# Moving the first loads of a one-layer decoder kernel: x's columns to another DMA queue, x's rows behind the second projection's weights

## The chip, the cores and the metric

The kernel runs on one core of one Trainium2 chip. The metric is the device time of one execution in microseconds (us), lower is better; it was run three times, and the median counts.

## The reference

One decoder layer on a sequence of 256 tokens with 1024 channels, in float32:

```python
h = rmsnorm(x, mix_norm_g)                       # x: (256, 1024)
proj = h @ w_in                                  # 1024 x 5632: qa ka va | qd kd vd | qm | three gates
qa, ka, qd, kd = rope(rmsnorm per head, positions)   # 64 wide heads; qm only normed
mem_n = rmsnorm(mem, mem_norm_g); mk, mv = mem_n @ w_mem_kv
o_a = block attention(qa, ka, va) @ w_branch_moba    # 6 heads
o_d = dilated attention(qd, kd, vd) @ w_branch_dil   # 6 heads
o_m = attention(qm, mk, mv) @ w_branch_mem           # 4 heads, 256 memory tokens
x = x + (sig(g0) * o_a + sig(g1) * o_d + sig(g2) * o_m) @ w_out
u = causal depthwise conv(rmsnorm(x) @ w_ffn_up)     # 1024 x 5632
x = x + (silu(u_gate) * u_val) @ w_ffn_down          # 2816 x 1024
```

The rotary part needs cos and sin of position times inverse frequency, and the dilated attention a table of counts, which is a constant.

## The kernel before

**Precision.** Every weight is read once, as float32, and split on the chip in two parts: `hi`, a rounded copy made on ACT, and `lo`, the remainder, made on DVE (some later on ACT with a DMA that accumulates). The activations are split the same way. A product is three matmuls: hi by hi, hi by lo, lo by hi.

**Columns and rows of x.** TensorE contracts over the partitions, so it needs x with channels on the partitions. The host gives x in that form too (`x_cols`, eight slabs `k` of 128 channels by 256 tokens, 128 KB each). `column_task` multiplies slab k with the norm's gain (ACT: `T_x` hi, DVE: `T_x` lo). The projections start from these and do without the mean square; that comes from the rows (`xs`, two tiles of 128 tokens, 512 KB each), squared and summed by `sums`, made into 1/rms by `rstd_task` (DVE, then POOL), and multiplied in afterwards: `head_scale_task` makes it for the head norms, `v_task` applies it as `va` and `vd` leave PSUM, and `row_scale_task` spreads it over all partitions with a matmul (`tp_Rx`) into `R`, which the gates take. `mem` goes the same way, with columns (`T_mem`) and rows.

**Weights.** They come in pieces through a ring of six raw buffers (`NRAW`): five pieces for `va` (one slab, one, two, two, two), four of 384 KB each for `vd`, `qa`, `ka` and so on, 512 KB for gates. `load` issues a piece on SP's queue as soon as the piece six before it is split. The order of the projections is written out in `ORDER`: va vd qa G0 ka G1 G2 mv mk ....

**Order.** A planner (`Order`) keeps an estimated clock for each engine, and issues next the stage that can start first by it, the one with the lower priority number among those close together. Each engine then runs its instructions in that order. `Stage("dve", 18.0)` means: not before 18 on the planner's clock. Where the planner expects TensorE to idle early on, `keep_busy` puts in small matmuls without use (`warm_...`, named by the time at which the planner expects the next one).

**First loads.** They are issued by hand, all on SP's queue, in the order of `LOADS`: x01 is slabs 0 to 1, `g` the gains, `w` the next weight piece, r0 and r1 the rows of x, `c` three loads: `cst` (the counts and the inverse frequencies), the positions and the head gains `hg`. What follows is planned: `mem_task` at 16 issues the convolution's weights, and mem's columns and rows; `rope_task` from 18 makes the rotary tables (19 small DVE operations on `rt`, three sines on ACT, then tables `ropeA` and `ropeB`); `mask_task` from 20.

Of the kernel before, what the change touches and what calls it, by code (L numbers as in the profile page):

```python
# [20 lines left out]
P = 128  # L21
# [16 lines left out]
RAW = 3  # L38
PRIO_SCALE = 11
CUTS = (0, 1, 2, 4, 8)  # L40
LOADS = "x01 g w x12 w x24 w x46 w x68 w r0 r1 c"
SUMS = (4, 130, 5)
BACK = (1.5, 2.0)
SLACK = 0.6
MEM_AT = 16.0
PRIO_SPLIT = (0, 0, 0, 12, 12, 22, 35, 40)
MAGIC = 12582912.0
TWO_PI = float(np.nextafter(np.float32(2.0 * np.pi), np.float32(0.0)))
# [185 lines left out]
def tile_layer(ctx: ExitStack, tc: tile.TileContext, io, out):  # L234
# [170 lines left out]


    xs = cpool.tile([P, NT, D], F32, tag="xs", name="xs")
    gcol = cpool.tile([P, 3, KT], F32, tag="gcol", name="gcol")
    cst = cpool.tile([P, 288], F32, tag="cst", name="cst")
    pos_i = cpool.tile([P, NT], I32, tag="pos_i", name="pos_i")  # L410
    hg = cpool.tile([P, 6, DH], F32, tag="hg", name="hg")
    conv = cpool.tile([P, 2 * NF, 4], F32, tag="conv", name="conv")
    ident = cpool.tile([P, P], F32, tag="ident", name="ident")
# [4 lines left out]
    maskf = cpool.tile([P, 512], F32, tag="maskf", name="maskf")  # L418
    A = cpool.tile([P, 4, NT, DH], F32, tag="ropeA", name="ropeA")
    B = cpool.tile([P, 4, NT, DH], F32, tag="ropeB", name="ropeB")  # L420
    cnt, invf = cst[:, 0:256], cst[:, 256:288]

    task = {}

# [35 lines left out]
    def head_scale_task(key, t):  # L460

        yield from rstd_task(key, t)
        rs = rstd[key, t]
        yield Stage("dve")
        dve.tensor_scalar(rs[:, 1:2], rs[:, 0:1], rs[:, 0:1], 1.0 / DH, op0=ALU.mult, op1=ALU.mult)
# [50 lines left out]


    def mask_task():
        yield Stage("dve", 20.0)
        dve.memset(maskf[:, 0:128], 0.0)  # L520
        dve.tensor_scalar(maskf[:, 128:256], cnt[:, 128:256], 0.0, NEG, op0=ALU.is_equal, op1=ALU.mult)
        dve.tensor_scalar(maskf[:, 256:512], cnt, 0.0, NEG, op0=ALU.is_equal, op1=ALU.mult)

    def rope_task():

        N = NT * HALF
        rt = apool.tile([P, 16, N], F32, tag="pT", name="rt", bufs=2)
        a, r, rc, sn, ns, cs, fr = (rt[:, k] for k in range(7))
        a12, acc, it, f0, f1 = (rt[:, k:k + 2].rearrange("p a n -> p (a n)") for k in (7, 9, 11, 13, 3))
        a1, a2 = rt[:, 7], rt[:, 8]  # L530
        posf = cpool.tile([P, NT], F32, tag="posf", name="posf")
        shape = [P, NT, HALF]
        yield Stage("dve", 18.0)
        dve.tensor_copy(posf, pos_i)
        yield Stage("dve")
        dve.tensor_mul(a.rearrange("p (t f) -> p t f", t=NT), invf.unsqueeze(1).to_broadcast(shape),
                       posf.unsqueeze(2).to_broadcast(shape))
        yield Stage("dve")
        dve.tensor_copy(a1.bitcast(F32R), a)
        yield Stage("dve")  # L540
        dve.tensor_sub(a2, a, a1)
        for d in range(3):
            yield Stage("dve")
            dve.tensor_scalar(it.bitcast(I32), a12, INV_2PI[d], None, op0=ALU.mult)
            yield Stage("dve")
            dve.scalar_tensor_tensor((acc, f0, f1)[d], a12, INV_2PI[d], it.bitcast(I32), op0=ALU.mult,
                                     op1=ALU.subtract)
        for f in (f0, f1):
            yield Stage("dve")
            dve.tensor_add(acc, acc, f)  # L550
        for d in (3, 4):
            yield Stage("dve")
            dve.scalar_tensor_tensor(acc, a12, INV_2PI[d], acc, op0=ALU.mult, op1=ALU.add)
        yield Stage("dve")
        dve.tensor_add(r, rt[:, 9], rt[:, 10])
        yield Stage("dve")
        dve.tensor_scalar(fr, r, MAGIC, MAGIC, op0=ALU.add, op1=ALU.subtract)
        yield Stage("dve")
        dve.tensor_sub(r, r, fr)
        yield Stage("dve")  # L560
        dve.tensor_scalar(rc, r, 0.25, None, op0=ALU.add)
        yield Stage("dve")
        dve.tensor_scalar(fr, rc, MAGIC, MAGIC, op0=ALU.add, op1=ALU.subtract)
        yield Stage("dve")
        dve.tensor_sub(rc, rc, fr)
        yield Stage("act")
        act.activation(ns, r, AF.Sin, scale=-TWO_PI)
        act.activation(sn, r, AF.Sin, scale=TWO_PI)
        act.activation(cs, rc, AF.Sin, scale=TWO_PI)
        yield Stage("dve")  # L570
        hq = hg.rearrange("p (a b) d -> p a b d", b=2)[:, :, 0, :]
        dve.tensor_scalar(hq, hq, DH ** -0.5, None, op0=ALU.mult)
        shape = [P, 4, NT, HALF]
        tab = {n: v.rearrange("p (t f) -> p t f", t=NT).unsqueeze(1).to_broadcast(shape)
               for n, v in (("cs", cs), ("sn", sn), ("ns", ns))}
        for hh in range(2):
            lo, hi = slice(hh * HALF, (hh + 1) * HALF), slice((1 - hh) * HALF, (2 - hh) * HALF)
            yield Stage("dve")
            dve.tensor_mul(A[:, :, :, lo], tab["cs"], hg[:, 0:4, lo].unsqueeze(2).to_broadcast(shape))
            yield Stage("dve")  # L580
            dve.tensor_mul(B[:, :, :, lo], tab["sn" if hh else "ns"], hg[:, 0:4, hi].unsqueeze(2).to_broadcast(shape))
# [476 lines left out]


    def mem_task():  # L1060
        yield Stage("pool", MEM_AT)
        nc.sync.dma_start(conv, io["conv"])
        cols = sig[:, KT:2 * KT, :]
        rows = sig[:, 2 * KT:3 * KT, :].rearrange("p a b -> p (a b)").rearrange("p (t n) -> p t n", t=NT)
        there = []
        for out_, in_ in [(cols[:, 0:4], io["mem_cols"][:, 0:4]), (cols[:, 4:8], io["mem_cols"][:, 4:8])] + \
                [(rows[:, t, :], io["mem"][t * P:(t + 1) * P, :]) for t in range(NT)]:
            nc.sync.dma_start(out_, in_)
            at["dma"] = max(at["dma"], od.t["pool"] + 1.15) + 1.5
            there.append(at["dma"] + 1.4)  # L1070
        columns_of("mem", 2, cols, 15, lambda k: there[k // 4])
        for t in range(NT):
            sums(rows[:, t, :], "mem", t, 16, [(0, 512, "act", there[2 + t]), (512, 1024, "act", there[2 + t])])
            task["rs", "mem", t] = od.add(head_scale_task("mem", t), 14)

    def keep_busy(start):

# [11 lines left out]
    with tc.manual_schedule():  # L1089
        nc.vector.memset(ones, 1.0)  # L1090
        nc.gpsimd.memset(mhalf, -0.5)
        warm = cpool.tile([P, 1], F32, tag="warm", name="warm")
        nc.scalar.activation(warm, mhalf[:, 0:1], AF.Square)
        xcol = sig[:, 0:KT, :]
        at["dma"] = 1.9
        there = {}
        for w in LOADS.split():
            if w == "g":
                nc.sync.dma_start(gcol, io["gcol"])
                at["dma"] += 0.06  # L1100
            elif w == "w":
                load(0.0, at["raw"] + 1)
            elif w == "c":
                nc.sync.dma_start(cst, io["cst"])
                nc.sync.dma_start(pos_i, io["pos"])
                nc.sync.dma_start(hg.rearrange("p k d -> p (k d)"), io["head_gains"].to_broadcast([P, 6 * DH]))
                at["dma"] += 1.4
            elif w[0] == "x":
                k0, k1 = int(w[1]), int(w[2])
                nc.sync.dma_start(xcol[:, k0:k1, :], io["x_cols"][:, k0:k1, :])  # L1110
                at["dma"] += 0.38 * (k1 - k0)
                for k in range(k0, k1):
                    there[k] = at["dma"] + 1.2
            else:
                t = int(w[1])
                nc.sync.dma_start(xs[:, t, :], io["x"][t * P:(t + 1) * P, :])
                at["dma"] += 1.5
                there["r", t] = at["dma"] + 1.3
        load(0.0)
        make_identity(nc, ident)  # L1120
        T["x"] = tpool.tile([P, KT, 2, S], F32R, tag="T8", name="T_x")
# [3 lines left out]
        warm_up = ps.tile([P, 512], F32, tag="acc", name="warm_up", bufs=4)  # L1125
        for i in range(WARM):
            nc.tensor.matmul(warm_up[:, :P], ones, ones, start=True, stop=True)
        for t in range(NT):
            r = there["r", t]
            sums(xs[:, t, :], "x", t, 9, [(0, 512, "act", r), (512, 1024, "dve", r)])  # L1130
            task["rs", "x", t] = od.add(head_scale_task("x", t), 8)
            task[f"R{t}"] = od.add(row_scale_task("x", t), 9)
        columns_of("x", 0, xcol, 2, lambda k: there[k])
        od.add(split_hi(), urgency(0))
        at["left"] = len(grains)
        od.add(split_lo("dve"), urgency(1))
        od.add(split_lo("sum"), 35)
        task["mask"] = od.add(mask_task(), 25)
        od.add(mem_task(), 15)
        task["rope"] = od.add(rope_task(), 18)  # L1140
        for b in range(3):
            task[("sig", b)] = od.add(sig_task(b), 28)
        od.add(spine(units), 50)
# [3 lines left out]
            od.run(task[key])  # L1147


def _constants():  # L1150
    i = np.arange(P)[:, None]
    j = np.arange(P)[None, :]
    c = []
    for base in (P, 0):
        d = base + i - j
        n = ((d >= 0) & (d <= 128)).astype(np.float32) + ((d >= 0) & (d % 4 == 0)) + ((d >= 0) & (d % 16 == 0))
        c.append(n.astype(np.float32))
    inv = (10000.0 ** (-np.arange(HALF) / HALF)).astype(np.float32)
    return np.concatenate(c + [np.broadcast_to(inv, (P, HALF))], axis=1).astype(np.float32)


# [36 lines left out]
```

## Time and profile before

| | |
|---|---|
| median of 3 runs | 419.19 us (418.9 to 419.26) |
| the profiled execution | 419.38 us |
| its span | 417.6 us, 7771 instructions |
| TensorE's granted clock | 1.00 of full speed throughout |
| TensorE matmul busy | 407.9 us, 98% of the span |
| DVE, ACT, POOL busy | 302.7, 269.1, 62.3 us |
| HBM read | 72.80 MB |

The profile is of one execution; times in it count from the first instruction. PE is TensorE's matmuls, PEld its weight loads, SPq the queue from which DMAs are issued. Matmuls without use count as busy. L101 is the line of the planner's helper, so operations are told apart by the tiles' names (`acc_va` is the accumulator of `va`).

### The profile page before, as it was taken

How to read it: one execution, taken by the hardware profiler on the slowest of the kernel's cores; microseconds unless marked ns; L12 is line 12 of the kernel's file. 1: busy time of each engine (PE TensorE's matmuls, PEld its weight loads, DVE VectorE, ACT ScalarE, POOL GpSimd, SP SyncE). 2: the span in 40 equal slices, each digit the busy share in tenths (PEclk: the TensorE clock that was granted, in tenths of full speed). 3: DMA queues.
4: the chain of work that ended last, by engine and by line, in shares of the span. 5: the costliest groups of instructions: out<-in, count | busy, mean ns of one | idle time of the engine just before them, and what ended most of it. 6: DMA issues, size and time to landing. Idle time of an engine off the chain costs nothing.

```text
span 417.6 us, 7771 instructions
## 1 busy us (share of the span) xinstructions
PE 407.9 (98%) x2968; PEld 384.0 (92%) x2968; DVE 302.7 (72%) x600; ACT 269.1 (64%) x448; POOL 62.3 (15%) x63
## 2 busy tenths in 40 slices
PE   8899999999999999999999989999999999999996
PEld 7799999989898999999889889999999999888996
DVE  2699986586786586367987999999998778545301
ACT  4699756768976665956577877766668776433300
POOL 0101534113424102322007200000000000000000
PEclk9999999999999999999999999999999999999999
DMA  6999986667677777577597659666799688664001
GB/s 198 383 374 278 317 249 157 181 167 180 146 200 162 201 208 197 131 228 239 140 290 177 162 131 287 188 187 201 230 257 222 230 220 239 204 197 150 0 2 50
DMA packets 97988, 83.12 MB, mean 199 GB/s; under 512 B 3104, under 2 KB 85920, under 8 KB 97952
## 3 DMA queue, kind: packets, MB, share of 16 engines
q1 hardware_dynamic: 95360, 73.86, 58.6%
q0 software_dynamic: 2592, 8.78, 11.7%
q8 instruction: 23, 0.38, 0.4%
q14 instruction: 13, 0.11, 0.1%
HBM read 72.80 MB, written 1.05 MB: 177 GB/s over the span
## 4 chain that ended last, share of the span: by engine, by line
PE 83%; DVE 8%; ACT 3%; DMA 2%; issue 2%; SPq 1%; DVEq 0%; ACTq 0%
PE acc_u L101 27%; PE acc_g L101 16%; PE acc_d L101 15%; PE acc_o L101 5%; PE acc_qd L101 2%; PE acc_kd L101 2%; DMA xs<-x 2%; PE acc_ba L101 2%; PE acc_bd L101 2%; PE sc L101 2%; PE po L101 2%; PE acc_mk L101 1%; PE acc_qm L101 1%; PE acc_bm L101 1%; PE acc_mv L101 1%
## 5 line engine op out<-in xcount | busy, mean ns | idle before, releaser
L101 PE MATMUL acc_u<-T_h,hi_up 128*128 128x256 f32 x512 | 91.4, 282 | 0.0
L101 PEld LDWEIGHTS acc_u<-T_h,hi_up 128*128 128x128 f32 x512 | 78.9, 189 | 0.0
L101 PE MATMUL acc_u<-T_h,lo_up 128*128 128x256 f32 x256 | 72.1, 282 | 0.0
L101 PE MATMUL acc_g<-T_x,hi_gate 128*128 128x256 f32 x384 | 71.8, 287 | 0.0
L101 PEld LDWEIGHTS acc_g<-T_x,hi_gate 128*128 128x128 f32 x384 | 59.6, 191 | 2.4 <-issue 2.2
L101 PE MATMUL acc_d<-hi_dn,gT 128*128 128x512 f32 (+1 forms) x220 | 57.0, 348 | 0.0
L101 PE MATMUL acc_g<-T_x,lo_gate 128*128 128x256 f32 x192 | 54.2, 282 | 0.0
L101 ACT ACTIVATE hi_up<-raw_up 128x1024 fp32r<-128x1024 f32 x44 | 46.0, 1054 | 4.3 <-DMA raw_up<-w_ffn_up 1.7
L101 PEld LDWEIGHTS acc_u<-T_h,lo_up 128*128 128x128 f32 x256 | 48.4, 189 | 0.0
L101 DVE TENSOR_TENSOR lo_up<-raw_up,hi_up 128x1024 fp32r<-128x1024 f32 x39 | 47.6, 1232 | 0.0
L101 DVE SCALAR_TENSOR_TENSOR y<-acc_u,conv,y 128x255 f32<-128x255 f32 x88 | 42.2, 481 | 7.3 <-ACT y L101 5.4
L101 PEld LDWEIGHTS acc_d<-hi_dn,gT 128*128 128x128 f32 x220 | 38.5, 189 | 5.5
L101 PE MATMUL acc_d<-lo_dn,gT 128*128 128x512 f32 (+1 forms) x110 | 38.3, 348 | 0.0
L101 DVE TENSOR_TENSOR lo_dn<-raw_dn,hi_dn 128x1024 fp32r<-128x1024 f32 x21 | 25.7, 1224 | 17.3 <-ACT hi_dn L101 17.3
L101 ACT ACTIVATE hi_dn<-raw_dn 128x1024 fp32r<-128x1024 f32 x22 | 23.3, 1057 | 22.4 <-PE acc_d L101 22.4
L101 PE MATMUL acc_u<-T_hu,hi_up 128*128 128x256 f32 x192 | 34.9, 284 | 2.6 <-DVE y L101 2.6
L101 PEld LDWEIGHTS acc_g<-T_x,lo_gate 128*128 128x128 f32 x192 | 36.7, 191 | 0.0
L101 DVE TENSOR_TENSOR lo_gate<-raw_gate,hi_gate 128x1024 fp32r<-128x1024 f32 x19 | 23.8, 1262 | 13.3 <-ACT hi_gate L101 12.8
L101 PEld LDWEIGHTS acc_u<-T_hu,hi_up 128*128 128x128 f32 x192 | 29.6, 189 | 2.9 <-ACT T_h L101 2.9
L101 ACT ACTIVATE y<-acc_u,conv 128x256 f32<-128x256 f32 x44 | 24.4, 561 | 10.9 <-PE acc_u L101 10.3
L101 ACT ACTIVATE hi_gate<-raw_gate 128x1024 fp32r<-128x1024 f32 x24 | 25.0, 1056 | 6.1 <-PE acc_qm L101 2.9
L101 PE MATMUL acc_u<-T_hu,lo_up 128*128 128x256 f32 x96 | 27.1, 282 | 0.0
(279 smaller groups left out, 850.9 us busy)
## 6 DMA issues: line engine op xcount, KB each, us to landing
raw_up<-w_ffn_up SPq DMA_DIRECT2D x44, 512.0 KB, 5.1
raw_gate<-w_in SPq DMA_DIRECT2D x24, 512.0 KB, 5.2
raw_dn<-w_ffn_down SPq DMA_DIRECT2D x22, 512.0 KB, 4.4
raw_wo<-w_out SPq DMA_DIRECT2D x8, 512.0 KB, 5.2
lo_gate<-raw_gate POOLq DMA_DIRECT2D x5, 512.0 KB, 5.1
lo_up<-raw_up POOLq DMA_DIRECT2D x5, 512.0 KB, 5.0
raw_vd<-w_in SPq DMA_DIRECT2D x4, 384.0 KB, 6.6
raw_qa<-w_in SPq DMA_DIRECT2D x4, 384.0 KB, 7.7
```

The lines of the kernel that those rows point to most:

```text
L101: return fn(*args, **kw)
```

## The change

The slabs of x are issued from ACT's queue, ahead of ACT's first operation, with slabs 4 to 8 as one load; six weight pieces, the first of `vd` among them, follow each other on SP. The rows of x are issued by a task of their own, `row_task`, once nine pieces (all of `va` and `vd`) have been issued; the counts and head gains come behind them. Mem's columns come at 24 and its rows at 28, both only after x's rows. Positions and inverse frequencies travel with the gains in the first small load, and `rope_task` may start at 5 with a higher priority; its last part, which needs the head gains, waits for 21.

```diff
-LOADS = "x01 g w x12 w x24 w x46 w x68 w r0 r1 c"
+LOADS = "x01 g w x12 w x24 w x48 w w w"
-MEM_AT = 16.0
+MEM_AT = 24.0
+MEM_ROWS_AT = 28.0
+ROWS_AT = 9
+ROPE_AT = 5.0
+CONST_AT = 21.0
...
+    small = cpool.tile([P, 3 * KT + HALF + NT], F32, tag="small", name="small")
+    gcol = small[:, :3 * KT].rearrange("p (g k) -> p g k", g=3)
+    invf, pos_i = small[:, 3 * KT:3 * KT + HALF], small[:, 3 * KT + HALF:].bitcast(I32)
+    cnt = cpool.tile([P, 256], F32, tag="cnt", name="cnt")
...
     def mask_task():
-        yield Stage("dve", 20.0)
+        yield Stage("dve", CONST_AT)
...
     def rope_task():
-        yield Stage("dve", 18.0)
+        yield Stage("dve", ROPE_AT)
...
         act.activation(cs, rc, AF.Sin, scale=TWO_PI)
-        yield Stage("dve")
+        yield Stage("dve", CONST_AT)
...
     def mem_task():
-        yield Stage("pool", MEM_AT)
+        yield Stage("pool", MEM_AT, lambda: 0.0 if task["rows"]["end"] else None)
...
+    def mem_rows_task():
+        yield Stage("pool", MEM_ROWS_AT, lambda: 0.0 if task["rows"]["end"] else None)
...
+    def row_task():
+
+        yield Stage("pool", lambda: 0.0 if at["raw"] >= ROWS_AT else None)
         for t in range(NT):
+            nc.sync.dma_start(xs[:, t, :], io["x"][t * P:(t + 1) * P, :])
+            at["dma"] = max(at["dma"], od.t["pool"] + 1.15) + 1.4
+            there = at["dma"] + 1.3
+            sums(xs[:, t, :], "x", t, 9, [(0, 512, "act", there), (512, 1024, "dve", there)])
+            task["rs", "x", t] = od.add(head_scale_task("x", t), 8)
+            task[f"R{t}"] = od.add(row_scale_task("x", t), 9)
+        nc.sync.dma_start(cnt, io["cnt"])
+        nc.sync.dma_start(hg.rearrange("p k d -> p (k d)"), io["head_gains"].to_broadcast([P, 6 * DH]))
+        at["dma"] += 1.4
...
-        nc.scalar.activation(warm, mhalf[:, 0:1], AF.Square)
...
-                nc.sync.dma_start(gcol, io["gcol"])
+                nc.sync.dma_start(small, io["small"])
...
-            elif w == "c":
-                nc.sync.dma_start(cst, io["cst"])
-                nc.sync.dma_start(pos_i, io["pos"])
-                nc.sync.dma_start(hg.rearrange("p k d -> p (k d)"), io["head_gains"].to_broadcast([P, 6 * DH]))
...
-                nc.sync.dma_start(xcol[:, k0:k1, :], io["x_cols"][:, k0:k1, :])
+                nc.scalar.dma_start(xcol[:, k0:k1, :], io["x_cols"][:, k0:k1, :])
...
+        nc.scalar.activation(warm, mhalf[:, 0:1], AF.Square)
...
+        task["rows"] = od.add(row_task(), 1)
...
-        task["rope"] = od.add(rope_task(), 18)
+        od.add(mem_rows_task(), 15)
+        task["rope"] = od.add(rope_task(), 11)
```

## Rows read from the trace of the kernel before

**Rows 1.** Busy time by stretch: the start, and what follows it

```profile
0.00:22.00 22.00, 18.74 (x104) 16.64 (x104) 11.35 (x28) 12.58 (x25) 2.23 (x9) 1.00 0.89 295
22.00:44.00 22.00, 22.00 (x142) 22.00 (x142) 21.28 (x55) 19.60 (x36) 1.10 (x2) 1.00 1.00 323
```

**Rows 2.** Timeline of TensorE, 10 to 66 us: start, us, what, idle before it

```profile
10.47 0.44 PE L101 MATMUL acc_va<-hi_va,T_x 128*128 128x384 f32 x1
...
13.94 0.45 PE L101 MATMUL acc_va<-lo_va,T_x 128*128 128x384 f32 x1
...
17.89 0.34 PE L101 MATMUL acc_va<-hi_va,T_x 128*128 128x384 f32 x1
18.93 0.49 PE L101 MATMUL tp_Rx<-diag_x,ones 128*128 128x128 f32 x2 [0.71 <-DVE diag_x L101]
19.26 1.06 PE L1086 MATMUL m_16.205137333333333_279<-ones 128*128 128x128 f32 x8
...
21.73 0.42 PE L101 MATMUL acc_vd<-hi_vd,T_x 128*128 128x384 f32 x1
...
30.24 0.33 PE L101 MATMUL acc_qa<-hi_qa,T_x 128*128 128x384 f32 x1
...
44.31 0.34 PE L101 MATMUL acc_ka<-hi_ka,T_x 128*128 128x384 f32 x1
...
52.42 0.55 PE L101 MATMUL tp_qa<-ident,t_qa 128*128 128x128 f32 x3 [0.66 <-DVE t_qa L101]
...
65.69 0.28 PE L101 MATMUL acc_mv<-hi_mv,T_mem 128*128 128x256 f32 x1
```

**Rows 3.** Timeline of ACT, 0 to 21 us

```profile
0.74 1.28 ACT L1093 ACT_TABLE_LOAD   x1 [0.74 <-PEq L1190]
...
9.57 0.84 ACT L101 ACTIVATE hi_va<-raw_va 128x768 fp32r<-128x768 f32 x1 [0.17 <-DMA raw_va<-w_in]
11.03 0.91 ACT L101 ACTIVATE T_x<-sig,gcol 128x256 fp32r<-128x256 f32 x2 [0.62 <-DMA sig<-x_cols]
...
15.06 0.63 ACT L101 ACTIVATE junk_x<-xs 128x512 bf16<-128x512 f32 x1 [0.43 <-DMA xs<-x]
...
19.63 0.57 ACT L101 ACTIVATE v_va<-acc_va,rs_x 128x384 f32<-128x384 f32 x1
20.10 0.84 ACT L101 ACTIVATE hi_vd<-raw_vd 128x768 fp32r<-128x768 f32 x1
```

**Rows 4.** Timeline of SP's queue, the issues: start, us

```profile
4.00 0.47 SPq L1110 DMA_DIRECT2D sig<-x_cols  x1
...
12.04 3.43 SPq L301 DMA_DIRECT2D raw_vd<-w_in  x4
```

**Rows 5.** Waits of SP's queue: us, times, longest

```profile
SPq L1104 <- DMA sig<-x_cols: 0.9, 1, 0.9
```

**Rows 6.** DMA issues from 12 to 17 us: KB each, us to landing

```profile
raw_vd<-w_in SPq DMA_DIRECT2D x4, 384.0 KB, 6.6
```

**Rows 7.** Stretches; the last two columns are DMA share and GB/s

```profile
0.00:4.00 4.00, 2.94 (x14) 2.94 (x15) 0.24 (x2) 2.00 (x3) 0.74 (x7) 1.00 0.41 110
4.00:6.00 2.00, 2.00 (x10) 1.69 (x10) 1.37 (x3) 0.92 (x2) 0.00 (x0) 1.00 0.66 168
6.00:8.00 2.00, 1.27 (x6) 0.68 (x6) 0.56 (x1) 0.52 (x1) 0.00 (x0) 1.00 0.90 227
8.00:10.00 2.00, 2.00 (x16) 2.00 (x17) 0.88 (x2) 1.34 (x3) 0.00 (x0) 1.00 1.02 336
10.00:12.00 2.00, 1.35 (x8) 0.90 (x7) 1.38 (x3) 1.32 (x3) 0.00 (x0) 1.00 1.06 403
12.00:18.00 6.00, 5.89 (x34) 5.47 (x32) 4.82 (x13) 3.63 (x7) 0.94 (x1) 1.00 1.05 380
```

**Rows 8.** Busy time of the rotary tables' operations alone (DVE, ACT)

```profile
22.00:40.00 18.00, 4.50 (x19) 0.00 (x0) 1.00 1.01 334
```

**Rows 9.** Timeline of DVE: the first remainder of ka's weights

```profile
38.18 0.95 DVE L101 TENSOR_TENSOR lo_ka<-raw_ka,hi_ka 128x768 fp32r<-128x768 f32 x1
```

More of the change, by code (lines that the diff above doesn't have):

```diff
@@ L407, in tile_layer @@
     xs = cpool.tile([P, NT, D], F32, tag="xs", name="xs")
-    gcol = cpool.tile([P, 3, KT], F32, tag="gcol", name="gcol")
-    cst = cpool.tile([P, 288], F32, tag="cst", name="cst")
-    pos_i = cpool.tile([P, NT], I32, tag="pos_i", name="pos_i")
+    small = cpool.tile([P, 3 * KT + HALF + NT], F32, tag="small", name="small")
+    gcol = small[:, :3 * KT].rearrange("p (g k) -> p g k", g=3)
+    invf, pos_i = small[:, 3 * KT:3 * KT + HALF], small[:, 3 * KT + HALF:].bitcast(I32)
+    cnt = cpool.tile([P, 256], F32, tag="cnt", name="cnt")
     hg = cpool.tile([P, 6, DH], F32, tag="hg", name="hg")
@@ L420, in tile_layer @@
     B = cpool.tile([P, 4, NT, DH], F32, tag="ropeB", name="ropeB")
-    cnt, invf = cst[:, 0:256], cst[:, 256:288]
     task = {}
@@ L1060, in mem_task @@
     def mem_task():
-        yield Stage("pool", MEM_AT)
+        yield Stage("pool", MEM_AT, lambda: 0.0 if task["rows"]["end"] else None)
         nc.sync.dma_start(conv, io["conv"])
         cols = sig[:, KT:2 * KT, :]
+        there = []
+        for k in (0, 4):
+            nc.sync.dma_start(cols[:, k:k + 4], io["mem_cols"][:, k:k + 4])
+            at["dma"] = max(at["dma"], od.t["pool"] + 1.15) + 1.5
+            there += [at["dma"] + 1.4] * 4
+        columns_of("mem", 2, cols, 22, lambda k: there[k])
@@ L1064, in mem_task @@
+    def mem_rows_task():
+        yield Stage("pool", MEM_ROWS_AT, lambda: 0.0 if task["rows"]["end"] else None)
         rows = sig[:, 2 * KT:3 * KT, :].rearrange("p a b -> p (a b)").rearrange("p (t n) -> p t n", t=NT)
[L1065 to L1068, printed above, removed]
+        for t in range(NT):
+            nc.sync.dma_start(rows[:, t, :], io["mem"][t * P:(t + 1) * P, :])
@@ L1069, in mem_task @@
             at["dma"] = max(at["dma"], od.t["pool"] + 1.15) + 1.5
-            there.append(at["dma"] + 1.4)
-        columns_of("mem", 2, cols, 15, lambda k: there[k // 4])
-        for t in range(NT):
-            sums(rows[:, t, :], "mem", t, 16, [(0, 512, "act", there[2 + t]), (512, 1024, "act", there[2 + t])])
-            task["rs", "mem", t] = od.add(head_scale_task("mem", t), 14)
+            there = at["dma"] + 1.4
+            sums(rows[:, t, :], "mem", t, 23, [(0, 512, "act", there), (512, 1024, "act", there)])
@@ new lines, in mem_rows_task @@
+            task["rs", "mem", t] = od.add(head_scale_task("mem", t), 14)
+    def row_task():
+        yield Stage("pool", lambda: 0.0 if at["raw"] >= ROWS_AT else None)
+        for t in range(NT):
+            nc.sync.dma_start(xs[:, t, :], io["x"][t * P:(t + 1) * P, :])
[7 more added lines that the diff above has]
+        at["dma"] += 1.4
@@ L1102, in tile_layer @@
                 load(0.0, at["raw"] + 1)
-            elif w == "c":
-                nc.sync.dma_start(cst, io["cst"])
-                nc.sync.dma_start(pos_i, io["pos"])
-                nc.sync.dma_start(hg.rearrange("p k d -> p (k d)"), io["head_gains"].to_broadcast([P, 6 * DH]))
-                at["dma"] += 1.4
             elif w[0] == "x":
                 k0, k1 = int(w[1]), int(w[2])
-                nc.sync.dma_start(xcol[:, k0:k1, :], io["x_cols"][:, k0:k1, :])
+                nc.scalar.dma_start(xcol[:, k0:k1, :], io["x_cols"][:, k0:k1, :])
                 at["dma"] += 0.38 * (k1 - k0)
@@ L1113, in tile_layer @@
                     there[k] = at["dma"] + 1.2
[L1114 to L1118, printed above, removed]
+        nc.scalar.activation(warm, mhalf[:, 0:1], AF.Square)
         load(0.0)
@@ L1127, in tile_layer @@
             nc.tensor.matmul(warm_up[:, :P], ones, ones, start=True, stop=True)
[L1128 to L1132, printed above, removed]
         columns_of("x", 0, xcol, 2, lambda k: there[k])
+        task["rows"] = od.add(row_task(), 1)
         od.add(split_hi(), urgency(0))
@@ L1147, in tile_layer, with _counts @@
             od.run(task[key])
-def _constants():
+def _counts():
     i = np.arange(P)[:, None]
@@ L1157, in _constants, with _inverse_frequencies @@
         c.append(n.astype(np.float32))
-    inv = (10000.0 ** (-np.arange(HALF) / HALF)).astype(np.float32)
-    return np.concatenate(c + [np.broadcast_to(inv, (P, HALF))], axis=1).astype(np.float32)
+    return np.concatenate(c, axis=1).astype(np.float32)
+def _inverse_frequencies():
+    return (10000.0 ** (-np.arange(HALF) / HALF)).astype(np.float32)
 def kernel(x, mem, positions, mix_norm_g, mem_norm_g, w_in, moba_q_norm_g, moba_k_norm_g, dil_q_norm_g,
@@ L1175 @@
         "mem_cols": arr(np.asarray(mem).reshape(S, KT, P).transpose(2, 1, 0)),
-        "pos": arr(np.asarray(positions).reshape(NT, P).T),
-        "gcol": arr(np.stack([np.asarray(g).reshape(KT, P).T for g in (mix_norm_g, ffn_norm_g, mem_norm_g)], axis=1)),
+        "small": arr(np.concatenate(
+            [np.asarray(g).reshape(KT, P).T for g in (mix_norm_g, ffn_norm_g, mem_norm_g)] +
+            [np.broadcast_to(_inverse_frequencies(), (P, HALF)), np.asarray(positions).reshape(NT, P).T.copy().view(np.float32)],
+            axis=1)),
         "head_gains": arr(np.concatenate([np.asarray(g).reshape(1, DH) for g in (
@@ L1181 @@
                                     np.asarray(ffn_conv_b).reshape(1, 2 * NF, P)], axis=0).transpose(2, 1, 0)),
-        "cst": _constants(),
+        "cnt": _counts(),
     }
```

## The prediction

> **What bounds the kernel now.** I read the stretches first, then TensorE's timeline, then who it waits for, then the queue and the DMA rate behind that. TensorE is the bound almost everywhere: from 22 to 44 us it is busy without a gap [rows 1], and the page gives it 98% of the span. So a change of the loads pays only where TensorE stands still or does matmuls without use, and that is in the first 22 us; its clock is granted in full there (1.00), so less filler is not replaced by a slower clock, as long as real work takes its place.
>
> There the reader is to see two losses [rows 2]. First, the matmuls of va: 48 at 0.174 us (the pace of vd: 30.24 - 21.73 = 8.51 us for 48, with a small filler at its front) would take 8.35 us, but those of slabs 2 to 7, three quarters of them, start at 10.47 and end only at 18.23. The last wait in them ends at 13.94, on slabs 4 and 5, after which they run through. Second, from 18.23 to 21.73, 3.50 us, TensorE has only the two small matmuls for R and filler: vd's first weights are not split. Why not: ACT takes `hi_vd` at 20.10, behind R and `v_va`, which hang on the rows of x [rows 3], and the weights were late anyway. They were issued at 12.04 and took 6.6 us to land, so about 18.6 [rows 4, 6]. The issue was late because `cst`, the positions and `hg` stood ahead of it on SP, and issues there wait for older loads to land (0.9 us in front of `cst`, for a pair of x's slabs [rows 5], which was issued eight places before it).
>
> **The bytes.** By the rates of [rows 7] the DMAs had moved 0.44 MB at 4 us, 0.78 at 6, 1.23 at 8, 1.90 at 10, 2.71 at 12 and 4.99 at 18. A load is usable some time after its last byte: counting KB in the order of issue, weights piece 2 (for slabs 2 and 3) ends at 1.32 MB, which is 8.3 us, and was used at 9.57; slabs 4 and 5 end at 1.59 MB, 9.1 us, and were used at 11.03 [rows 3]. So 1.3 to 2.0 us. The early rate is low (168 and 227 GB/s against 336 to 403 later) with the engines' share at 0.66 and 0.90, although the queue was full: slabs 4 and 5 were issued at 4.00 [rows 4] and used 7 us later.
>
> **The change, part by part.**
>
> *vd's weights ahead of rows, counts, gains: the gap goes.* Order on SP is now: small load 29 KB, five pieces of va (1536 KB), vd's first (384 KB), with x's 1024 KB on ACT's queue. vd's first piece ends at 2973 KB = 3.04 MB, which the present curve reaches at 12.9 us, so it lands near 15, instead of 18.6. The other three wait for ring buffers that va frees by 12 us or so, and end at 4.22 MB, 16.0 us, landing at 18. TensorE needs them at 19 and later, 2.1 us apart. ACT and DVE have room: 12.58 and 11.35 us busy of 22 [rows 1]. Gain 3.50 us, less the R matmuls, which now stand inside vd's stream; I take 0.5 us for them, by the 0.49 us of the first pair [rows 2] and an overlap with their neighbours. Net -3.0.
>
> *x's slabs on a second queue: when does va end?* This is the term that I can't read off, since no load here is issued from ACT. If both queues move equal bytes, piece 2 ends at twice 797 KB = 1.63 MB instead of 1.32, and all of x at 2.10 MB; slabs 4 to 8 are one load, so slab 4 waits for the whole: 2.10 MB instead of 1.59. On the present curve that is 10.5 us instead of 9.1, so va's last wait and its end come 1.4 us later. If the second queue gave the rate of 10 to 12 us (403 GB/s) from 4 us on, 2.10 MB is there at 8.1 us and va ends 0.9 us earlier. Between them: the second queue fills what the engines left idle. 168 GB/s at a share of 0.66 becomes 260 at 1.02, 227 at 0.90 becomes 257; that is 0.24 MB more by 8 us, or 0.65 us at the rate that follows. Then va ends 1.4 - 0.65 = 0.8 us later than now, at 19.0. I take that, because the idle share is in the rows, while the bytes per busy share were low too, so that a full rate from the start is far.
>
> The Trainium skill (DMA: Bandwidth & Descriptors, "Issuing engines are not separate DMA queues") says that DMAs issued by several engines run on the same 16 DMA engines and that issuing from more than one saves only the sequencer's time. By that rule the curve stays as it is and va ends 1.4 us later, which is the first rival below; the backlog of 7 us speaks for it, the share of 0.66 against it.
>
> *ACT's issues ahead of its table load.* Four issues at about 0.47 us [rows 4] move the table load (0.74, 1.28 us [rows 3]) to about 2.6 us, and the first `T_x` behind it to about 4.1. Were the issues of both engines to stand in one line, it would be 5.9. Neither reaches TensorE's bound: the 12 matmuls of slabs 0 and 1 take 2.1 us and must be done by 10.5, when those of slabs 2 and 3 start [rows 2]. Cost 0; with va's loads 2 us faster it would be up to 1.
>
> *Rows of x later.* Through them 5149 KB = 5.27 MB are moved; the curve is there at 18.8 us, so they land near 20.5. From first square to first R matmul it was 15.06 to 18.93, to `v_va` 19.63 [rows 2, 3]: now R at about 24, `v_va` at 25. What waits behind them: `v_va` frees va's accumulators, which qa needs when vd ends, at 19.0 + 8.35 + 0.5 = 27.9. So 3 us of cover, cost 0. qa's weights, 1.61 MB with counts and gains ahead by 0.33, end at 7.2 MB, near 24 us at 380 GB/s, landing by 26; also in time, the last not needed before 34.
>
> *Rotary tables early, mem later.* Their 19 DVE operations, 4.50 us [rows 8], now lie where DVE waits (11.35 of 22 us busy) instead of where it is full (21.28 of 22) [rows 1]. The sines bring a table load of 1.28 us by the first one's duration, on ACT, ahead of vd's splits, which have 4 us of lead: 0. Later it gives something: TensorE waits 0.66 us for `t_qa` at 52.42 [rows 2], which is late since DVE is full and the tables were not there when qa ended. That should go: -0.7 (bound: 0). Mem is used from 65.69 us on [rows 2]; moving it lets qa's pieces pass, and costs nothing.
>
> **Is it kept?** From 22 us on TensorE must be fed 3 us earlier. ka's first remainder was ready at 39.1 and used at 44.31 [rows 2, 9], 5 us ahead; DVE gains 4.5 us by the tables. So yes.
>
> **Sum.** -3.50 + 0.5 + 0.8 - 0.7 = -2.9 us on the profiled 419.38 (span 417.6, 1.8 us around it). The runs' median is 419.19, 0.2 lower, so 416.3; with what the planner's other order gives, 416.2.
>
> **Rivals.**
> 1. *The second queue adds no rate.* va ends 1.4 us later: -3.50 + 0.5 + 1.4 - 0.7 = -2.3, so 416.9. For it: the queue was full. Against: idle engines.
> 2. *Full rate early.* va ends 0.9 us earlier: -4.6, so 414.6. Against it: bytes per busy share, which more queueing doesn't mend.
> 3. *Slower: R's matmuls block TensorE.* The planner runs ahead of the chip: a filler meant for 16.2 ran at 19.26 [rows 2]. If it puts the R matmuls early in vd's stream, TensorE stands in front of them until about 24 while vd's weights lie ready. At vd's very beginning (19.0) that costs 5 us: 416.2 + 5 = 421.2. It decides from the point where TensorE waits 3 us, so with R placed before 21, among vd's first 12 matmuls. Against it: the planner is as early for va's loads, and keeps the rows behind all of vd's.
> 4. *Given back.* Weights or DVE can't follow in 22 to 44 us, where DVE is full and DMA at 1.00 [rows 1], and the wait reappears in qa or ka: 419. Against it: ka's lead.
>
> **Chances.** Main course 0.38, rival 1 0.27, rival 2 0.15, rival 3 0.11, rival 4 0.09. About 0.2%, 0.8 us, is what a measurement tells from no change: faster 0.80, same 0.09, slower 0.11. The range takes in rivals 1 and 2 with 1 us for the new order of everything behind, and part of rival 4: 413.6 to 418.8.
>
> **What would show it.** `acc_vd` following `acc_va` without filler, at 18 to 20 us; `acc_qa` starting near 28 instead of 30.24; a DMA share near 1.0 from 4 to 8 us (main) or still 0.7 (rival 1); R inside vd's stream without idle before it; no wait before `tp_qa`. I am wrong if TensorE waits before `tp_Rx` or at qa's start, or if `acc_ka` starts no earlier than 44.

## The result

The kernel after takes 416.36 us (median of four runs, 415.56 to 416.88), the one before 419.15 beside it (418.9 to 419.26): a ratio of 0.993, 95% interval 0.9914 to 0.9945, so 2.8 us faster, where the sum of the prediction had 2.9. Forecast 416.2, range 413.6 to 418.8. The profiled execution of the kernel after took 416.41 us, span 414.6, against 419.38 and 417.6 before; TensorE is busy 406.4 us of it, 407.9 before. Two executions of variants below, of 1012.96 and 440.99 us, were disturbed: they count in those variants' medians but not in the ratios, and the trace of the first is not used.

TensorE's timeline of the kernel after, which answers to [rows 2] (start, us, what, idle before it):

```profile
5.81 0.69 PE L105 MATMUL acc_va<-hi_va,T_x 128*128 128x384 f32 x1 [0.54 <-ACT hi_va L105]
6.40 0.69 PE L105 MATMUL acc_va<-lo_va,T_x 128*128 128x384 f32 x1
6.89 0.84 PE L105 MATMUL acc_va<-hi_va,T_x 128*128 128x384 f32 x2
...
10.21 1.54 PE L1110 MATMUL warm_8.807152_184<-ones 128*128 128x128 f32 x12
11.50 0.42 PE L105 MATMUL acc_va<-hi_va,T_x 128*128 128x384 f32 x1
...
18.13 0.33 PE L105 MATMUL acc_va<-hi_va,T_x 128*128 128x384 f32 x1
18.30 0.33 PE L105 MATMUL acc_vd<-hi_vd,T_x 128*128 128x384 f32 x1
...
23.50 0.38 PE L105 MATMUL tp_Rx<-diag_x,ones 128*128 128x128 f32 x2
...
24.79 0.39 PE L105 MATMUL tp_Rx<-diag_x,ones 128*128 128x128 f32 x2
...
27.14 0.33 PE L105 MATMUL acc_qa<-hi_qa,T_x 128*128 128x384 f32 x1
...
41.20 0.34 PE L105 MATMUL acc_ka<-hi_ka,T_x 128*128 128x384 f32 x1
...
50.43 0.52 PE L105 MATMUL tp_qa<-ident,t_qa 128*128 128x128 f32 x3 [0.69 <-DVE t_qa L105]
...
62.61 0.28 PE L105 MATMUL acc_mv<-hi_mv,T_mem 128*128 128x256 f32 x1
```

The reader is to see that vd's first matmul (18.30) stands directly behind va's last (18.13), and that R's two pairs (23.50, 24.79) stand inside vd with no idle before them. qa begins 3.10 us earlier than before, ka 3.11, mv 3.08; the span is 3.0 shorter. So all of the gain is made in the first 27 us, and it stays. The one thing that should have changed later and did not is the wait ahead of `tp_qa`: 0.69 us, 0.66 before.

ACT in the same execution, which answers to [rows 3]; ACTq is its queue, from which x's slabs are now issued:

```profile
0.74 1.86 ACTq L1128 DMA_DIRECT2D sig<-x_cols  x4
2.62 1.28 ACT L1132 ACT_TABLE_LOAD   x1 [2.62 <-issue]
...
9.73 0.84 ACT L105 ACTIVATE hi_va<-raw_va 128x768 fp32r<-128x768 f32 x1 [1.14 <-DMA raw_va<-w_in]
10.48 1.29 ACT L105 ACTIVATE T_x<-sig,small 128x256 fp32r<-128x256 f32 x3
...
13.56 2.33 ACT L105 ACTIVATE hi_vd<-raw_vd 128x768 fp32r<-128x768 f32 x3
...
20.92 0.58 ACT L105 ACTIVATE v_va<-acc_va,rs_x 128x384 f32<-128x384 f32 x1 [0.30 <-POOL rs_x L105]
```

`hi_vd` starts at 13.56 instead of 20.10, with no wait for its load. The weights for slabs 2 and 3 (9.73) come no earlier than before (9.57), but slabs 4 to 6 (10.48) need no wait, where there was one of 0.62 us.

Stretches of the kernel after, which answer to [rows 7]; the last two columns are DMA share and GB/s:

```profile
0.00:4.00 4.00, 2.94 (x14) 2.94 (x15) 0.17 (x1) 1.36 (x2) 0.74 (x7) 1.00 0.51 86
4.00:6.00 2.00, 1.46 (x7) 1.16 (x6) 0.70 (x2) 1.29 (x4) 0.00 (x0) 1.00 0.88 277
6.00:8.00 2.00, 2.00 (x6) 1.70 (x7) 0.91 (x3) 0.88 (x3) 0.00 (x0) 1.00 1.00 383
8.00:10.00 2.00, 2.00 (x8) 1.74 (x7) 1.69 (x6) 0.86 (x3) 0.00 (x0) 1.00 1.04 393
10.00:12.00 2.00, 2.00 (x17) 2.00 (x16) 1.39 (x3) 2.00 (x5) 0.00 (x0) 1.00 1.06 373
```

Between 4 and 8 us the loads move 277 and 383 GB/s, where it was 168 and 227. The stretch from 6 to 8 us shows one thing more: six matmuls in 2.00 busy us, at a granted clock of 1.00.

### The profile page after: what moved, and what is told of

Read it like the earlier page. It is cut to its first block, busy times and chain, and to the rows that moved or that the text cites. A ratio compares the mean times of both kernels' runs of the same rounds, so it can differ in the third digit from the quotient of the medians.

```text
span 414.6 us, 7737 instructions
## 1 busy us (share of the span) xinstructions
PE 406.4 (98%) x2952; PEld 383.9 (93%) x2952; DVE 302.6 (73%) x601; ACT 270.9 (65%) x449; POOL 58.9 (14%) x62
## 4 chain that ended last, share of the span: by engine, by line
PE 91%; DVE 3%; ACT 3%; DMA 1%; issue 1%; SPq 0%; DVEq 0%; ACTq 0%
PE acc_u L105 27%; PE acc_g L105 16%; PE acc_d L105 15%; PE acc_o L105 5%; PE acc_va L105 3%; PE acc_qd L105 2%; PE acc_bd L105 2%; PE acc_ba L105 2%; PE acc_kd L105 2%; PE acc_vd L105 2%; PE acc_qa L105 2%; PE sc L105 2%; PE po L105 2%; PE acc_qm L105 1%; PE acc_mk L105 1%; PE acc_bm L105 1%
```

## The experiments

Ratios are to runs of the kernel before on the same chip, with a 95% interval. "A" and "B" in the expectations are the two theories set against each other for that run.

**The reordering without the second queue.** The kernel after with x's slabs on SP.

```diff
-                nc.scalar.dma_start(xcol[:, k0:k1, :], ...)
+                nc.sync.dma_start(xcol[:, k0:k1, :], ...)
```

> The changed kernel with one edit undone: the slabs of x are issued on SP's queue again, each at the place that the list of first loads gives it. Theory A, the second queue raises the early rate (277 and 383 GB/s at 4 to 6 and 6 to 8 us in the changed kernel, 168 and 227 before): the rate falls back to about 170 and 230, slabs 4 to 8 land near 11.4 us instead of 9.6, va ends about 1.2 us later than 18.46, and the time is about 417.5. Theory B, the rate came from larger loads and their order: the rate stays above 270 and 370, va ends no later, and the time is 416.4 or less.

Measured: 417.19 us, 0.9952 (0.9939 to 0.9964). The same kernel was run once more for its trace:

> The changed kernel with x's slabs on SP once more, for a profile at full clock, since the first profile of it fell in an execution in which TensorE ran at about half pace throughout. Theory A, the second queue is worth what va's end shows: 168 and 227 GB/s at 4 to 8 us, va ends about 0.9 us later than 18.46, vd follows it without filler, and everything behind keeps that distance; 417.2. Theory B, the 0.9 us are lost somewhere else and va ends at 18.5.

Measured: 417.16 us, 0.9952 (0.9935 to 0.9969), span 415.1. Stretches of this kernel:

```profile
4.00:6.00 2.00, 1.85 (x10) 1.50 (x10) 1.47 (x3) 1.03 (x2) 0.00 (x0) 1.00 0.74 157
6.00:8.00 2.00, 0.96 (x4) 0.38 (x3) 0.52 (x1) 0.52 (x1) 0.00 (x0) 1.00 0.99 244
```

and its TensorE:

```profile
18.35 0.33 PE L105 MATMUL acc_va<-hi_va,T_x 128*128 128x384 f32 x1
18.52 0.33 PE L105 MATMUL acc_vd<-hi_vd,T_x 128*128 128x384 f32 x1
...
50.88 0.52 PE L105 MATMUL tp_qa<-ident,t_qa 128*128 128x128 f32 x3 [0.92 <-DVE t_qa L105]
```

The gap between va and vd is gone here too: the change without its second queue, the order of the loads above all, closes it, and gives 1.8 to 1.9 of the 2.8 us. What the queue adds to that is near the noise: the two intervals (0.9939 to 0.9964 here, 0.9914 to 0.9945 for the kernel after) just overlap. The low early rate is back with x on SP (157 and 244 GB/s). Yet vd starts only 0.22 us later than in the kernel after; `tp_qa`'s wait is 0.23 longer, which makes the 0.5 us between the two spans.

**The second queue without the reordering.** The kernel before, x's five loads issued from ACT ahead of its first operation; then the same with four loads (slabs 4 to 8 as one).

```diff
-        nc.scalar.activation(warm, mhalf[:, 0:1], AF.Square)
...
-                nc.sync.dma_start(xcol[:, k0:k1, :], ...)
+                nc.scalar.dma_start(xcol[:, k0:k1, :], ...)
...
+        nc.scalar.activation(warm, mhalf[:, 0:1], AF.Square)
         load(0.0)
```

> The kernel before with one part of the change alone: its five loads of x's slabs on ACT's queue, ahead of ACT's first operation; rows, counts and positions stay ahead of vd's weights on SP. Theory A, the queue raises the rate: at 4 to 8 us 280 to 380 GB/s; vd's first weights land near 17 instead of 18.6, vd starts near 20 instead of 21.73, and the time is about 417.6. Theory B, it adds no rate: 168 and 227 GB/s as before, and 419.2. In both the gap between va and vd, with R's matmuls and filler, is still there.

Measured: 418.93 us, 0.9997 (0.9986 to 1.0007): no change; the profiled execution was one of the longer ones, 420.49. ACT in this kernel:

```profile
0.74 4.12 ACTq L1109 DMA_DIRECT2D sig<-x_cols  x5
4.89 1.28 ACT L1118 ACT_TABLE_LOAD   x1 [4.89 <-DMA sig<-x_cols]
...
6.69 0.51 ACT L101 ACTIVATE hi_va<-raw_va 128x384 fp32r<-128x384 f32 x1
```

Four issues took 1.86 us in the kernel after; five take 4.12, and what ends them is the landing of a slab of x. The trace's records of the issues tell why: the loads signal their landing on eight semaphores (counters on which engines wait), which are taken again from the program's ninth load on, and an issue that takes one again first waits for the load that had it before. The fifth slab load takes the semaphore of the first. So this is a wait of the program, not a limit of ACT's queue; it hurts here because all of ACT's work stands behind it. ACT then loads its table and splits the first weights 1.5 us later than in the kernel after. va starts at 7.25 us instead of 4.95 and ends at 20.28. So the rate (328 and 386 GB/s from 4 to 8 us) is paid for with a late start. Four loads:

```diff
-LOADS = "x01 g w x12 w x24 w x46 w x68 w r0 r1 c"
+LOADS = "x01 g w x12 w x24 w x48 w w r0 r1 c"
```

> The kernel before with the queue alone, done with four loads: slabs 4 to 8 as one, so that ACT's table load does not stand behind a fifth issue (in the run with five it started at 4.89 us, when the first load had landed). Theory A, the gain of the change is vd's early issue and the queue alone moves only va: va ends near 18.4 us, R and filler still stand ahead of vd, vd starts near 21.2, and the time is about 418.5. Theory B, the queue is the main part and the run with five loads hid it: 417.2 or less.

Measured: 418.29 us, 0.9984 (0.9975 to 0.9992). TensorE in this kernel:

```profile
18.16 0.33 PE L101 MATMUL acc_va<-hi_va,T_x 128*128 128x384 f32 x1
18.34 0.38 PE L101 MATMUL tp_Rx<-diag_x,ones 128*128 128x128 f32 x2
18.55 1.06 PE L1086 MATMUL rm_16.63656133333333_280<-ones 128*128 128x128 f32 x8
...
20.59 0.42 PE L101 MATMUL acc_vd<-hi_vd,T_x 128*128 128x384 f32 x1
```

va ends at 18.49 and vd starts at 20.59, 1.14 us earlier than before: the rows and vd's weights land sooner, but R and filler still stand between the projections. The two parts alone give 0.8 and 1.9 us; together, 2.8. They add up within what the runs tell.

**Cover of what was moved back: the rows of x.** The kernel after, with the rows issued behind six weight pieces instead of nine.

```diff
-ROWS_AT = 9
+ROWS_AT = 6
```

> The changed kernel with the rows of x, the counts and the head gains issued as soon as six weight pieces are out (ROWS_AT 6 instead of 9), so ahead of vd's second to fourth piece. Theory A, what closed the gap was that vd's first piece is issued at once and that R left the front of vd: vd's second piece lands near 18.2 us, its remainder is ready at 20, just before TensorE wants it at 20.4, and the time stays at 416.4 within 0.5. Theory B, all of vd's weights have to be ahead of the rows: TensorE waits 2 us or more inside vd, and the time is 418 to 419.

Measured: 419.5 us (417.08 to 423.13, twelve runs), 1.001 (0.9988 to 1.0031). All of the gain is lost, but not where the rows were moved: vd starts at 18.12 with R inside it, and ka at 41.66. It is lost here, on ACT:

```profile
34.37 3.31 ACT L105 ACTIVATE T_mem<-sig,small 128x256 fp32r<-128x256 f32 x8 [2.46 <-DMA sig<-mem_cols]
...
38.32 0.47 ACT L105 ACTIVATE sq_qa<-acc_qa 128x384 f32<-128x384 f32 x1
```

and then on TensorE (one line of its timeline, then stretches, in which the third number from the right is the granted clock):

```profile
52.46 0.52 PE L105 MATMUL tp_qa<-ident,t_qa 128*128 128x128 f32 x3 [1.97 <-DVE t_qa L105]
...
50.00:52.00 2.00, 0.49 (x3) 0.17 (x1) 1.97 (x6) 1.58 (x2) 0.96 (x1) 1.00 0.52 161
52.00:54.00 2.00, 1.54 (x9) 1.57 (x10) 2.00 (x4) 0.49 (x1) 0.00 (x0) 0.71 1.04 273
54.00:56.00 2.00, 2.00 (x12) 2.00 (x11) 2.00 (x3) 0.00 (x0) 0.00 (x0) 0.50 1.06 212
```

The planner orders mem's columns ahead of qa's squares on ACT; they come late, so `sq_qa` starts 1.7 us later than in the kernel after (36.60), `t_qa` with it, and TensorE waits 1.97 us before `tp_qa`. After this wait the granted clock falls to 0.50, the 1.2 GHz level, until 56 us. mv starts at 66.14, 3.5 us later than in the kernel after. The theory for the place was right, that for the time wrong.

**The wait before `tp_qa`.** First the rotary tables, moved back to where they were:

```diff
-ROPE_AT = 5.0
+ROPE_AT = 18.0
-        task["rope"] = od.add(rope_task(), 11)
+        task["rope"] = od.add(rope_task(), 18)
```

> The changed kernel with the rotary tables late again (from 18 on the planner's clock, with the old priority 18). Theory A, the early tables gave nothing, because TensorE still waits 0.69 us for t_qa in the changed kernel: 416.4 within 0.4. Theory B, they make the room on DVE without which TensorE could not be fed 3 us earlier: TensorE waits in qa, G0 or ka, and the time is 417 to 418.5.

Measured: 416.0 us, 0.9922 (0.9909 to 0.9935). Late tables cost nothing, and here there is no wait before `tp_qa` at all. Two things differ on ACT: it takes mem's columns at 33.95 us without waiting for them, and the planner put the second `sq_qa` ahead of the last squares of mem's rows (41.78 us). ACT in the kernel after, where it waits for the columns and the second `sq_qa` stands behind all four squares:

```profile
33.89 1.71 ACT L105 ACTIVATE T_mem<-sig,small 128x256 fp32r<-128x256 f32 x4 [0.69 <-DMA sig<-mem_cols]
35.78 0.91 ACT L105 ACTIVATE T_mem<-sig,small 128x256 fp32r<-128x256 f32 x2 [0.18 <-DMA sig<-mem_cols]
36.60 0.47 ACT L105 ACTIVATE sq_qa<-acc_qa 128x384 f32<-128x384 f32 x1
36.97 0.90 ACT L105 ACTIVATE T_mem<-sig,small 128x256 fp32r<-128x256 f32 x2
...
41.49 0.63 ACT L105 ACTIVATE junk_mem<-sig 128x512 bf16<-128x512 f32 x1
...
43.90 0.48 ACT L105 ACTIVATE sq_qa<-acc_qa 128x384 f32<-128x384 f32 x1
```

Second, mem's loads later still:

```diff
-MEM_AT = 24.0
-MEM_ROWS_AT = 28.0
+MEM_AT = 34.0
+MEM_ROWS_AT = 36.0
```

> The changed kernel with mem's columns and rows at 34 and 36 on the planner's clock instead of 24 and 28. Theory A, the wait of 0.69 us in front of tp_qa has stayed because mem's hi and lo parts took on ACT and DVE the room that the rotary tables left: it goes, and the time is about 415.7. Theory B, it hangs on something else, or mem is then late itself: 416.4 or more.

Measured: 420.78 us, 1.0036 (1.0022 to 1.0049), slower than before. The wait before `tp_qa` is gone, and another took its place. TensorE in this kernel:

```profile
65.48 0.58 PE L105 MATMUL acc_mv<-lo_mv,T_mem 128*128 128x256 f32 x1 [3.29 <-DMA lo_mv<-raw_mv]
```

The remainder of mv's first weights comes late: here the planner had it made by ACT and an accumulating DMA, issued at 58.3 us and landed 7.1 us later, where the kernel after makes it on DVE (53.40).

All profiles together say what the wait before `tp_qa` hangs on. In ten profiles of the kernel after and its variants, ACT waits for mem's columns ahead of qa's first squares in four: the kernel after (0.87 us), x on SP (0.68), slabs 4 to 8 on SP (0.69), the rows moved (2.46). TensorE waits before `tp_qa` in the same four: 0.69, 0.92, 0.46 and 1.97 us. In the other six there is neither wait (with mem later still, its columns come behind both of qa's squares). One of these six, the kernel after with seven matmuls at the start (below), has early tables and the kernel after's order on ACT, the second `sq_qa` behind all four squares. So neither the tables nor that order makes the wait; it goes with mem's columns, which stand ahead of qa's squares and land too late. Why they land in time in one profile and not in another stays open; and 24 and 28 leave mem less room to move than 10 us.

**How x's slabs are shared between the queues.** Slabs 4 to 8 back on SP, behind the weights for slabs 2 and 3:

```diff
-                nc.scalar.dma_start(xcol[:, k0:k1, :], ...)
+                (nc.scalar if k0 < 4 else nc.sync).dma_start(xcol[:, k0:k1, :], ...)
```

> The changed kernel with slabs 4 to 8 issued on SP instead of ACT's queue, behind va's third weight piece. Theory A, on ACT's queue these 512 KB take the engines from that piece, which landed at 9.73 us although the DMAs had moved 0.4 MB more by 8 us than before: the piece lands near 8.6, va ends near 17.4 instead of 18.46, and the time is about 415.4. Theory B, with less on the second queue the rate falls and nothing is won: the piece lands near 9.6 and the time is 416.4 or more.

Measured: 415.39 us, 0.991 (0.9898 to 0.9923), the lowest median of all, though its interval overlaps that of the kernel after. ACT in this kernel:

```profile
8.21 0.85 ACT L105 ACTIVATE hi_va<-raw_va 128x768 fp32r<-128x768 f32 x1 [0.33 <-DMA raw_va<-w_in]
9.50 0.91 ACT L105 ACTIVATE T_x<-sig,small 128x256 fp32r<-128x256 f32 x2 [0.44 <-DMA sig<-x_cols]
```

The weights for slabs 2 and 3 are there at 8.21 us instead of 9.73, which fits 512 KB of x no longer sharing the engines with them: 8.21 to 8.28 in the three profiles with this split, 9.33 to 10.09 in the six with all of x in four loads on ACT. vd starts at 16.73 instead of 18.30, and the span is 1.8 shorter. SP's queue in this kernel shows the wait for a semaphore once more, now on SP and with only three loads on ACT:

```profile
SPq L305 <- DMA sig<-x_cols: 1.5, 1, 1.5
```

The opposite, with slabs 4 to 8 in two loads, so five on ACT:

```diff
-LOADS = "x01 g w x12 w x24 w x48 w w w"
+LOADS = "x01 g w x12 w x24 w x46 w x68 w w"
```

> The changed kernel with slabs 4 to 6 and 6 to 8 as two loads again, five in all on ACT's queue. Theory A, ACT's fifth issue waits until its first load has landed, and the table load and all splits behind it: the table load starts near 4.9 us instead of 2.6, TensorE's first projection matmul at 7.2 instead of 5.8, va ends near 20, and the time is about 418. Theory B, the late start in the run of the queue alone had another cause: 416.4.

Measured: 416.72 us, 0.9942 (0.9925 to 0.996). Again the fifth issue waits for a slab to land: the five take 4.25 us, TensorE stands 2.11 us before va, and ka starts at 42.86, 1.66 later than in the kernel after. Half of it comes back at `tp_qa`, which does not wait here; mv is 0.82 later. The expected place was right, the expected time (about 418) was not. Slabs 4 to 8 on SP and late tables together:

```diff
-ROPE_AT = 5.0
+ROPE_AT = 18.0
...
-                nc.scalar.dma_start(xcol[:, k0:k1, :], ...)
+                (nc.scalar if k0 < 4 else nc.sync).dma_start(xcol[:, k0:k1, :], ...)
...
-        task["rope"] = od.add(rope_task(), 11)
+        task["rope"] = od.add(rope_task(), 18)
```

> The changed kernel with slabs 4 to 8 on SP and the rotary tables late, the two edits that did best alone (415.39 and 416.0). Theory A, they act in different places (va's end; the wait before tp_qa) and add: 415.0. Theory B, the room on DVE is needed once TensorE is fed 1.6 us earlier still, and a wait comes back in qa, G0 or ka: 415.8 or more.

Measured: 415.59 us, 0.992 (0.9906 to 0.9933). No sum of the two: the wait before `tp_qa` is gone, but in this profile va's first twelve matmuls took 0.32 us each, and vd started at 17.91.

**The pace of va's first matmuls.** In the kernel after the first twelve take 4.4 us (5.81 to 10.21), in the variant with slabs 4 to 8 on SP 2.6 (5.92 to 8.55), with the same granted clock of 1.00. Three more matmuls without use at the start, in both kernels:

```diff
-WARM = 4
+WARM = 7
```

> The kernel after with slabs 4 to 8 back on SP's queue, and seven matmuls without use at the start instead of four, so that TensorE is busy until about 5.8 us, when the first split weights are there. Theory A: the half pace of va's first matmuls (0.32 us each in the profile of the kernel after and in those of three variants, 0.174 in others) comes from the idle 0.5 to 1.2 us ahead of them; with TensorE busy up to then they run at 0.174 us, va ends at 16.9 or before, and the times lie close together, at 414.6 to 415.0. Theory B: the pace has another cause; the first matmuls may run at 0.32 us here too, the median stays at 415.4 and the spread of 1.2 us with it; matmuls without use that run past 5.9 us only delay the start.

> The kernel after with seven matmuls without use at the start instead of four, and nothing else. Theory A: TensorE's idle 0.54 us ahead of va's first matmul goes, the first twelve run at 0.174 us instead of 0.32; but the weights for slabs 2 and 3 land at 9.7 us as before, so va ends no earlier than 18.3 and the median stays at 416.2 to 416.4. Theory B: the pace has another cause and stays at 0.32 in this profile; 416.4 likewise. The pace in the profile tells them apart, not the time.

Measured: 415.74 us, 0.9919 (0.9902 to 0.9935) with slabs 4 to 8 on SP, and 416.39, 0.994 (0.9917 to 0.9963) for the kernel after. TensorE in the first:

```profile
4.21 2.34 PE L1110 MATMUL warm_5.374288_138<-ones 128*128 128x128 f32 x10
6.20 0.67 PE L105 MATMUL acc_va<-hi_va,T_x 128*128 128x384 f32 x1
6.67 0.55 PE L105 MATMUL acc_va<-lo_va,T_x 128*128 128x384 f32 x1
7.05 0.51 PE L105 MATMUL acc_va<-hi_va,T_x 128*128 128x384 f32 x2
```

No idle stands before va, and the slow pace ends within its first two matmuls in one profile; in the other, none is slow. That fits the idle before va as its cause, in one profile of each; it doesn't prove it, since the slow pace varied between profiles already, and not with the length of the idle: 1.19 us stood ahead of the fast matmuls with slabs 4 to 8 on SP, 0.54 ahead of the slow ones in the kernel after. But the medians did not move, and the times lie no closer together (414.41 to 416.38): the theory that this pace makes the spread falls. In the kernel after with seven, the weights for slabs 2 and 3 land at 10.09 us and vd starts at 18.60, later than at 18.30 with the slow pace: there the landing decides.

## Why the prediction was right, step by step

**The gap between va and vd: right.** Forecast to go whole, it did, and it does so without the second queue (417.16 us). vd's weights were forecast to land near 15 us; their split started at 13.56.

**R's matmuls in vd's stream: right, a little cheaper.** 0.5 us was taken; vd takes 8.84 us (18.30 to 27.14) instead of 8.51, so 0.33. R ran at 23.50 (24 forecast), and `v_va` in time for qa. Rival 3, R ahead of its data, did not come, not even with the rows moved (R at 19.16 with no idle).

**The end of va: the term that was mis-sized.** "0.8 us later than now" became 0.2 (last matmul 18.13 instead of 17.89). The step that failed is that the second queue only "fills what the engines left idle": 260 and 257 GB/s were taken for 4 to 8 us, 277 and 383 came. By the rates of the kernel after, the 2.10 MB of the prediction's count are there near 9.1 us instead of 10.5 on the old curve; so the 1.4 us of sharing is just paid back. That reversed the reason given against rival 2: the bytes per busy share did rise, to 383 GB/s at a share of 1.00, against 244 at 0.99 with x on SP. The last wait was another too: slab 4 needed none (10.48), and va's end hung on the weights for slabs 2 and 3 (9.73, after a wait of 1.14 us). The twelve matmuls of slabs 0 and 1 took 4.4 us where 2.1 were counted; with the fast pace, in the kernel after with seven matmuls at the start, vd began no earlier (18.60). It did not become rival 2, since from 0 to 4 us less was moved (86 GB/s, 110 before), and slabs 4 to 8 still shared with the weights that va needed next. The variants that take them away show that price: vd starts 1.57 and 1.25 us earlier, and 0.39 in the profile with slow first matmuls; the medians differ by 1.0 us, with intervals that overlap.

The Trainium skill (DMA: Bandwidth & Descriptors, "Issuing engines are not separate DMA queues") says that issuing from several engines saves only the sequencer's time. The traces here don't agree for this stretch: 157 and 244 GB/s with x on SP, 277 and 383 with it on ACT, everything else alike. The sequencer's time is not the reason: with x on SP, loads of 1.34 MB had been issued by 4.0 us and 1.27 MB had moved by 8.0. Rival 1 is refuted in its rate. What makes the single queue slow early on was not tried.

**`tp_qa`: wrong.** "That should go: -0.7" did not come: 0.69 us remain. The reason given, that tables built early unburden DVE at qa's end, fell: with late tables the wait was absent. In the kernel after, mem's columns, moved to later by the same change, stand ahead of qa's squares on ACT and land too late; "costs nothing" for mem was the step that missed this. The ten profiles bear it out: TensorE waits in those four in which ACT waits for these columns, and in no other.

**The sum.** -3.50 + 0.33 + 0.2 + 0 = -3.0, which is the difference of the spans (417.6 to 414.6); the medians differ by 2.8. The forecast had +0.8 and -0.7 in the places of 0.2 and 0: two misses of 0.6 and 0.7 us that cancelled. That the number came so near is luck; its main term, the gap, is not.

**Kept: right, and narrower than thought.** ka's 3.11 us of lead stayed to the end. But rival 4's mechanism is real close by: moving the rows or mem costs all of the gain, through a wait at `tp_qa` or mv that the start does not show.

## What to carry to other kernels

When a stall has a chain of loads behind it, count bytes in the order of issue and put what is needed next first; that gave two thirds of the gain here. A second queue is worth trying where the early rate is low, but see which of its issues must wait for an older load, since the engine's own work stands behind them, and leave the large load that isn't urgent behind the one that is. A task moved "off the path" has to be followed on each engine to where it now stands: mem's columns came to stand ahead of qa's squares, and where they landed late TensorE waited.

## What the runs showed of the hardware that was not expected

- Early loads ran faster when issued from two engines: 266 to 336 GB/s from 4 to 6 us and 374 to 398 from 6 to 8 in all profiles with x, or half of it, on ACT, 157 to 168 and 227 to 244 in the two with all on SP. From 6 to 8 us the engines' share was 0.99 in one of these and 1.00 in the kernel after, for 244 and 383 GB/s.
- The same 128x384 matmuls took 0.174 us each in some profiles and 0.32 in others from 6 to 10 us, with the granted clock shown as 1.00 in both. Their ratio, 1.84, is near that of 128x256 matmuls at the two levels of the clock (0.215 us at a granted 0.50, 0.12 at 1.00, at 66 and 70 us with mem later); that the clock was low there without a record of it is an argument, not shown.
- After a wait of 1.97 us before `tp_qa` the granted clock went to 0.50 (0.71 from 52 to 54 us, 0.50 from 54 to 56, 1.00 again from 57), and after one of 3.29 us before mv's matmuls likewise (0.50 from 66 to 68). So these waits cost more than their own length.
